# Second feed-forward layer's in-projection by a Strassen product of seven multiplications, from the fifth tile on

## The chip, the core and the metric

The kernel runs on one core of a Trainium2 chip. The core has a matrix engine (TensorE, PE in the profile; PEld is its weight loading), a vector engine (VectorE, DVE), a scalar engine (ScalarE, ACT), a general engine (GpSimd, POOL) and a queue engine that mostly issues transfers (SyncE, SP). POOL and ACT have transfer queues of their own. The metric is the device time of one execution in microseconds (us).

## The reference

One layer of a hybrid decoder on 512 tokens of width 1024, all in float32:

```python
x = x + 0.5 * swiglu_ffn(rmsnorm(x, ffn1_norm), ffn1_w_in, ffn1_w_down)
...
x = x + 0.5 * swiglu_ffn(rmsnorm(x, ffn2_norm), ffn2_w_in, ffn2_w_down)
...
return rmsnorm(h, final_norm)

def swiglu_ffn(x, w_in, w_down):
    a, b = jnp.split(x @ w_in, 2, axis=-1)
    return (jax.nn.silu(a) * b) @ w_down
```

Between the two feed-forward layers (FFN1, FFN2) stand three parallel branches (a state-space model, windowed attention, attention to a memory). The change concerns FFN2, the last stage. Its in-projection multiplies the normalised x (512 x 1024) by a weight matrix of 1024 x 5632: 2816 columns for the gate half a and 2816 for the value half b. The down-projection has 2816 x 1024.

## The kernel before

Activations lie transposed, features on the 128 partitions and the 512 tokens (T) along the rows: `xT[k]` is x's k-th block of 128 features, `uh[k]` and `ul[k]` are the high and low parts (type float32r) of x times the norm's gain. A float32 product is made of three float32r matmuls, high x high, high x low and low x high, which add up in PSUM.

`split` makes the two parts of a block of weights (128 x 1024 numbers): ACT copies it to `wh` (line 124), DVE subtracts to get `wl` (line 125); `split_plain` does the same for activations (lines 143 and 144). `mm_T` (lines 133 to 135) makes one output tile of 128 x 512: 8 blocks of features by three matmuls, 24 matmuls of 512 columns, with a block of weights as the stationary operand and u as the moving one.

The 2816 hidden features are 22 tiles of 128, taken two at a time: `ffn_in(w, f, ...)` makes the tiles f and f + 1. SP loads two chunks of 1 MB through `load_chunk` (two buffers `wraw`), one for the gate and one for the value columns; for each tile there is a product `pa` and a product `pb`, 96 matmuls for the pair. Then comes the gating: DVE multiplies `pa` by the row `rb`, 1 / rms of each token (line 307), ACT takes tanh, DVE forms a (1 + tanh) (310) and multiplies by `pb` (313 in FFN2), and the result is split into `gh` and `gl`, the moving operands of the down-projection. FFN2 leaves r out of the value half; `down2` multiplies by it later, as `rq` = r / 4 of each token.

The tiles form groups, (0, 6), (6, 6), (12, 6), (18, 4) as (first, number). `down2` of a group runs after the first pair of the next group; it accumulates four PSUM tiles `dn0` to `dn3` for each half of the output columns and adds them into `x2n`, x with tokens on the partitions. `natural_x2` makes `x2n` after the first group: 32 transposes on PE (line 1079) and 8 copies on ACT (line 1080).

The program is written in this order, but a scheduler with a priority and a timeline of its own sets each engine's order when the kernel is built. Each engine then works its row in order, and waits where an instruction waits. Transfers of SP's and POOL's queues are issued in the order of those rows too. One line of the main loop is to be kept in mind:

```python
ffn_in(ffn2_w_in, f, fp, g, True)
if f == f0 and pend is not None:
    down2(*pend, False)
```

Of the kernel before, what the change touches and what calls it, by code (L numbers as in the profile page):

```python
# [11 lines left out]
F32 = mybir.dt.float32  # L12
F32R = mybir.dt.float32r
# [7 lines left out]
P = 128  # L21
# [63 lines left out]
def kernel(ctx, tc, x, mem, ffn1_norm, ffn1_w_in, ffn1_w_down, mix_norm, w_in, a_re, a_im, log_dt,  # L85
# [56 lines left out]
    def split_plain(src, h, l, eng=V):  # L142
        S.activation(h, src, AF.Copy)  # L143
        eng.tensor_tensor(l, src, h.bitcast(F32), op=ALU.subtract)  # L144
# [140 lines left out]
    U = list(zip(uh, ul))  # L285


    def ffn_in(w, f, pool, g, late_r):

        begun = w is ffn1_w_in and f == 0  # L290
        if not begun:
            ra = load_chunk(w[0], 0, KD, f * P, 2 * P)
            rbk = load_chunk(w[0], 0, KD, FF + f * P, 2 * P)
        for j in range(2):
            if begun:
                pa, pb = first_ps[(0, j)], first_ps[(FF, j)]
            else:
                pa = ps_tile("mm")
                mm_T(pa, split(ra[:, :, j * P:(j + 1) * P]), U)
                if f + j == 0 and late_r:  # L300
                    norm_sums()
                pb = ps_tile("mm")
                mm_T(pb, split(rbk[:, :, j * P:(j + 1) * P]), U)
            if f + j == 0:
                norm_rows()
            a = pool.tile([P, T], F32, name="ff_a", tag="ff_a", bufs=2)
            V.tensor_tensor(a, pa, rows["r"], op=ALU.mult)  # L307
            t = pool.tile([P, T], F32, name="ff_t", tag="ff_t", bufs=2)
            S.activation(t, a, AF.Tanh, scale=0.5)
            V.scalar_tensor_tensor(a, t, 1.0, a, op0=ALU.add, op1=ALU.mult)  # L310
            b = pool.tile([P, T], F32, name="ff_b", tag="ff_b", bufs=2)
            if late_r:
                V.tensor_tensor(b, a, pb, op=ALU.mult)  # L313
            else:
                V.tensor_tensor(b, pb, rows["r"], op=ALU.mult)
                V.tensor_tensor(b, a, b, op=ALU.mult)
            split_plain(b, *g[f + j])

    def hidden(pool, f0, nf):
        return {f: (pool.tile([P, T], F32R, name="gh", tag="gh", bufs=8),  # L320
# [738 lines left out]
    mid.close()  # L1059


    ps_open("ps_c", 4, "mm")
    ctx.enter_context(ps_stack)
    fp = ctx.enter_context(sb_pool("ffn2"))
    x2 = [fp.tile([P, D], F32, name=f"x2n{r}") for r in range(4)]
    fnb = fp.tile([P, D], F32, name="fnb")
    nc.scalar.dma_start(fnb, bass.AP(tensor=final_norm.tensor, offset=final_norm.offset, ap=[[0, P], [1, D]]))
    ssq = fp.tile([P, 4, 3], F32, name="ssq")
    V.memset(ssq, 0.0)
    rq = fp.tile([P, 4], F32, name="rq")  # L1070
    g = {}

    def natural_x2():
        V.tensor_scalar(rq, r_nat, 0.25, None, op0=ALU.mult)
        for r in range(4):
            for hf in range(2):
                pt = ps_tile("mm")
                for k in range(4):
                    TE.transpose(pt[:, k * P:(k + 1) * P], xT[4 * hf + k][:, r * P:(r + 1) * P], ident)
                S.activation(x2[r][:, hf * T:(hf + 1) * T], pt, AF.Copy)  # L1080

    def down2(f0, nf, last):
        for hf in range(2):
            cols = slice(hf * T, (hf + 1) * T)
            pd = [ps_tile(f"dn{r}", 1) for r in range(4)]
            for f in range(f0, f0 + nf, 4):
                n4 = min(4, f0 + nf - f)
                raw = load_chunk(ffn2_w_down[0], f, n4, hf * T, T)
# [21 lines left out]
            for r in range(4):  # L1110

                for c in ((0, 256), (256, 512)) if last and hf == 1 and r == 3 else ((0, 512),):
                    sub = slice(*c)
                    xr = x2[r][:, hf * T:(hf + 1) * T][:, sub]
                    V.scalar_tensor_tensor(xr, pd[r][:, sub], rq[:, r:r + 1], xr, op0=ALU.mult, op1=ALU.add)
                    if last:
                        junk = fp.tile([P, T], F32, name="junk", tag="junk", bufs=2)
                        n = hf + c[0] // 256
                        S.activation(junk[:, sub], xr, AF.Square, accum_out=ssq[:, r, n:n + 1])
                if last and hf == 0:  # L1120
# [24 lines left out]
    def finish_rows(r, y):  # L1145
        dst = out.rearrange("(j r) d -> r j d", r=4)[r]
        if r < 2:
            G.tensor_scalar(x2[r][:, :T], x2[r][:, :T], y, None, op0=ALU.mult)
        else:
            S.activation(x2[r][:, :T], x2[r][:, :T], AF.Copy, scale=y)  # L1150
        nc.sync.dma_start(dst[:, :T], x2[r][:, :T])
        V.scalar_tensor_tensor(x2[r][:, T:], x2[r][:, T:], y, fnb[:, T:], op0=ALU.mult, op1=ALU.mult)
        nc.sync.dma_start(dst[:, T:], x2[r][:, T:])
# [45 lines left out]
```

## Time and profile before

| | |
|---|---|
| median of 3 runs | 1279.95 us (1278.78 to 1280.48) |
| profiled execution | 1280.05 us |
| its span, first to last instruction | 1278.3 us |
| mean granted TensorE clock | 0.997 |
| first row of the gating of FFN2 on DVE (ff_a, line 307) | 918.51 us |
| PE busy from 1270 us to the end | 0.68 us |

The profile is one execution, taken by the hardware profiler. In a timeline row stand the start and the length of an instruction (us), the engine, the line of the kernel, the operation, "result<-operands", the shape and a count; a bracket at its end is idle time before it and who ended it. Starts that lie closer than the length overlap: the step from start to start is then the price in a row of such instructions. In a row of waits stand who waited, for what, and in total us, how often, and the longest. A row on transfers ends with its count, its size and the median time from issue to landing. Shares of busy time alone say little here, since every stage has its own limit.

### The profile page before, as it was taken

The page shows a single profiled execution, that of the slowest core. Times are in us where ns is not written, and L with a number is a line of the kernel's source. Part 1 is how long each engine was busy: PE and PEld are TensorE (multiplying, and loading weights), DVE is VectorE, ACT ScalarE, POOL GpSimd, SP SyncE. Part 2 cuts the span into 40 slices and gives each one's busy share as a digit, 9 for nine tenths or more (in the row PEclk, how much of TensorE's full clock was granted, in tenths as well). Part 3 has the DMA queues.
Part 4 walks back from the last instruction along what each step waited for, and adds up shares of the span by engine and source line. Part 5 has one row for each costly group of instructions (what it writes and reads, how often), then busy time and mean ns, then how long its engine had stood idle before and what let it go on. Part 6 is the DMA issues. An engine that isn't in the chain of part 4 may idle for free.

```text
span 1278.3 us, 15573 instructions
## 1 busy us (share of the span) xinstructions
PE 1260.2 (99%) x6116; PEld 1036.3 (81%) x6116; DVE 723.1 (57%) x1405; ACT 417.9 (33%) x635; POOL 82.0 (6%) x67
## 2 busy tenths in 40 slices
PE   8999999999999999999999999999999999999997
PEld 6888888788889788898877777888888888888886
DVE  7999456966457477644436544455544354344444
ACT  4322222233335333324424443334323122122233
POOL 3000000000011034400000000002000000000002
PEclk9999999999999999999999999999999999999999
DMA  6233333745237746452227121344231323323221
GB/s 196 89 111 116 131 115 90 190 148 168 84 96 258 227 135 181 146 182 67 66 73 158 42 66 42 99 140 149 83 126 56 116 71 110 115 66 115 92 90 66
DMA packets 152961, 149.34 MB, mean 117 GB/s; under 512 B 27668, under 2 KB 136276, under 8 KB 152596
## 3 DMA queue, kind: packets, MB, share of 16 engines
q1 hardware_dynamic: 129136, 133.48, 33.4%
q10 hardware_dynamic: 23624, 14.61, 3.9%
q8 instruction: 48, 0.79, 0.3%
q0 software_dynamic: 128, 0.26, 0.1%
q14 instruction: 25, 0.20, 0.1%
HBM read 133.35 MB, written 16.16 MB: 117 GB/s over the span
## 4 chain that ended last, share of the span: by engine, by line
PE 93%; DVE 3%; DMA 2%; ACT 1%; issue 0%; SPq 0%; ACTq 0%
PE ps_mm L133 24%; PE ps_mm L134 24%; PE ps_mm L135 24%; PE ps_dn L1107 3%; PE ps_dn L1106 3%; PE ps_dn L1108 3%; PE ps_acc L884 1%; DMA wraw<-in_xattn_w_kv_dram 1%; DVE wl L125 1%; PE ps_mm L822 1%; PE ps_mm L821 1%; PE ps_mm L823 1%; PE ps_tr L877 1%; PE ps_acc L732 1%; DMA wraw<-in_ffn_w_in_dram 1%; PE ps_sc L864 1%
## 5 line engine op out<-in xcount | busy, mean ns | idle before, releaser
L124 ACT ACTIVATE wh<-wraw 128x1024 fp32r<-128x1024 f32 (+2 forms) x242 | 228.5, 946 | 655.0 <-PE ps_mm L134 469.5
L133 PE MATMUL ps_mm<-uh,wh 128*128 128x512 f32 x1024 | 402.2, 393 | 0.8 <-ACT uh L143 0.5
L134 PE MATMUL ps_mm<-ul,wh 128*128 128x512 f32 x1024 | 400.3, 391 | 1.6 <-DVE ul L144 1.6
L135 PE MATMUL ps_mm<-uh,wl 128*128 128x512 f32 x1024 | 400.2, 391 | 0.0
L125 DVE TENSOR_TENSOR wl<-wraw,wh 128x1024 fp32r<-128x1024 f32 (+2 forms) x242 | 269.2, 1114 | 172.8 <-ACT wh L124 166.9
L134 PEld LDWEIGHTS ps_mm<-ul,wh 128*128 128x128 f32 x1024 | 192.9, 188 | 41.7 <-DVE ul L144 1.9
L133 PEld LDWEIGHTS ps_mm<-uh,wh 128*128 128x128 f32 x1024 | 192.6, 188 | 42.0 <-ACT uh L143 0.9
L135 PEld LDWEIGHTS ps_mm<-uh,wl 128*128 128x128 f32 x1024 | 192.6, 188 | 41.2 <-issue 0.7
L307 DVE TENSOR_TENSOR ff_a<-ps_mm,rb 128x512 f32<-128x512 f32 x44 | 30.3, 689 | 89.0 <-PE ps_mm L135 89.0
L1107 PE MATMUL ps_dn<-wl,gh 128*128 128x512 f32 x176 | 70.2, 399 | 0.0
L134 PE MATMUL ps_mm<-gl,wh 128*128 128x512 f32 x176 | 70.1, 398 | 0.0
L133 PE MATMUL ps_mm<-gh,wh 128*128 128x512 f32 x176 | 69.8, 399 | 0.0
L135 PE MATMUL ps_mm<-gh,wl 128*128 128x512 f32 x176 | 69.7, 398 | 0.0
L1106 PE MATMUL ps_dn<-wh,gh 128*128 128x512 f32 x176 | 69.3, 394 | 0.0
L1108 PE MATMUL ps_dn<-wh,gl 128*128 128x512 f32 x176 | 68.8, 392 | 0.0
L217 POOL TENSOR_TENSOR sqacc<-sqacc,sqk 128x512 f32<-128x512 f32 x12 | 20.1, 1677 | 693.9 <-ACT sqk L216 693.8
L313 DVE TENSOR_TENSOR ff_b<-ff_a,ps_mm 128x512 f32<-128x512 f32 x22 | 15.1, 687 | 52.6 <-PE ps_mm L135 52.6
L1106 PEld LDWEIGHTS ps_dn<-wh,gh 128*128 128x128 f32 x176 | 33.0, 188 | 8.6
L133 PEld LDWEIGHTS ps_mm<-gh,wh 128*128 128x128 f32 x176 | 33.0, 188 | 8.1 <-issue 0.2
L135 PEld LDWEIGHTS ps_mm<-gh,wl 128*128 128x128 f32 x176 | 33.0, 188 | 8.0
L1108 PEld LDWEIGHTS ps_dn<-wh,gl 128*128 128x128 f32 x176 | 33.0, 188 | 7.8
L134 PEld LDWEIGHTS ps_mm<-gl,wh 128*128 128x128 f32 x176 | 33.0, 188 | 7.7
(327 smaller groups left out, 1606.1 us busy)
## 6 DMA issues: line engine op xcount, KB each, us to landing
wraw<-in_ffn_w_in_dram SPq DMA_DIRECT2D x42, 1024.0 KB, 5.1
wraw<-in_w_in_dram SPq DMA_DIRECT2D x25, 1024.0 KB, 5.3
wraw<-in_ffn_w_down_dram SPq DMA_DIRECT2D x12, 768.0 KB, 4.8
wraw<-in_ffn_w_down_dram SPq DMA_DIRECT2D x8, 1024.0 KB, 5.1
wraw<-in_ffn_w_down_dram SPq DMA_DIRECT2D x10, 512.0 KB, 3.6
wraw<-in_xattn_w_kv_dram SPq DMA_DIRECT2D x4, 1024.0 KB, 7.4
wraw<-in_ssm_w_glu_dram SPq DMA_DIRECT2D x8, 512.0 KB, 4.7
wraw<-in_w_out_dram SPq DMA_DIRECT2D x4, 1024.0 KB, 5.5
```

The source lines that it names most:

```text
L124: S.activation(h, raw, AF.Copy)
L125: eng.tensor_tensor(l, raw, h.bitcast(F32), op=ALU.subtract)
L133: TE.matmul(ps, h[:, k, :], rhs[k][0], start=first and k == 0, stop=False)
L134: TE.matmul(ps, h[:, k, :], rhs[k][1], start=False, stop=False)
L135: TE.matmul(ps, l[:, k, :], rhs[k][0], start=False, stop=last and k == n - 1)
L217: (V if k == KD - 1 else G).tensor_tensor(rows["sq"], rows["sq"], sq, op=ALU.add)
L307: V.tensor_tensor(a, pa, rows["r"], op=ALU.mult)
L313: V.tensor_tensor(b, a, pb, op=ALU.mult)
L732: TE.matmul(py[:, q * P:(q + 1) * P], lhsT.rearrange("p r c -> p (r c)"), rhs[:, q, :], start=t == 0, stop=t == 2)
L1106: TE.matmul(pd[r], gh[:, tok], h, start=st, stop=False)
L1107: TE.matmul(pd[r], gh[:, tok], l, start=False, stop=False)
L1108: TE.matmul(pd[r], gl[:, tok], h, start=False, stop=en)
```

## The change

For the tiles 4 to 21, nine of the eleven pairs, `fast_in` takes the place of `ffn_in`. The pair's product is seen as a matrix of 2 x 2 blocks: the weights by columns (gate or value) and by half of the 1024 features, u by half of the features and by left and right 256 tokens. Eight products of blocks become seven, with sums of weight blocks (s1 to s4) and of u blocks (t1 to t4), in Winograd's form: t1·s1, u·a11, u·a12, t2·s2, u·s4, t3·s3 and t4·q22, where a11 and a12 are the halves of the gate chunk and q22 is the lower half of the value columns. Each is made for two tiles by 4 blocks of features by three parts: 24 matmuls of 256 columns, 168 for the pair.

- The sums s1 and s3 come from two transfers of 512 KB each: SP loads one block, then POOL's queue adds the other block into the same tile (`accum_op`). The sums s2 and s4 are made by DVE. The blocks s1, s3, q22, s2 and s4 of all pairs share five buffers (`wq`).
- Seven blocks of 128 x 1024 are split for a pair, where four were.
- `combine_u` makes t1 to t4 and their high and low parts once, before tile 4, from x times gain times r; `own_u` writes the parts of u itself again, now with r in them; `natural_x2` moves to this place, and its tiles take the memory of `xT`.
- Partial products lie in halves of PSUM tiles; ACT copies some out (`ff_e` and halves of `ff_a`), DVE adds them. The gate half comes out negated, and tanh and the next step allow for it.
- r is now applied to the value half in `ffn_in`, by one more DVE operation for each tile of f < 4, and `down2` multiplies by the constant 0.25. PSUM has 8 tiles of one kind and no `dn` tiles. `ff_b` goes (`ff_t` is used again), and the load of the final norm moves behind the loop in the program.

```diff
-            a = pool.tile([P, T], F32, name="ff_a", tag="ff_a", bufs=2)
+            a = pool.tile([P, T], F32, name="ff_a", tag="ff_a", bufs=nbuf)
             V.tensor_tensor(a, pa, rows["r"], op=ALU.mult)
             t = pool.tile([P, T], F32, name="ff_t", tag="ff_t", bufs=2)
             S.activation(t, a, AF.Tanh, scale=0.5)
             V.scalar_tensor_tensor(a, t, 1.0, a, op0=ALU.add, op1=ALU.mult)
-            b = pool.tile([P, T], F32, name="ff_b", tag="ff_b", bufs=2)
-            if late_r:
-                V.tensor_tensor(b, a, pb, op=ALU.mult)
-            else:
-                V.tensor_tensor(b, pb, rows["r"], op=ALU.mult)
-                V.tensor_tensor(b, a, b, op=ALU.mult)
-            split_plain(b, *g[f + j])
+            V.tensor_tensor(t, pb, rows["r"], op=ALU.mult)
+            V.tensor_tensor(t, a, t, op=ALU.mult)
+            split_plain(t, *g[f + j])
...
-    ps_open("ps_c", 4, "mm")
+    ps_open("ps_c", 8, "mm")
...
     def natural_x2():
-        V.tensor_scalar(rq, r_nat, 0.25, None, op0=ALU.mult)
-        for r in range(4):
-            for hf in range(2):
+
+        for hf in range(2):
+            pts = []
+            for r in range(4):
                 pt = ps_tile("mm")
                 for k in range(4):
                     TE.transpose(pt[:, k * P:(k + 1) * P], xT[4 * hf + k][:, r * P:(r + 1) * P], ident)
-                S.activation(x2[r][:, hf * T:(hf + 1) * T], pt, AF.Copy)
+                pts.append(pt)
+            for r in range(4):
+                x2[r, hf] = xpool.tile([P, T], F32, name=f"x2n{r}{hf}", tag=f"xT{4 * hf + r}")
+                S.activation(x2[r, hf], pts[r], AF.Copy)
...
+    comb = [{n: fp.tile([P, 4, HT], F32R, name=f"{n}{z}") for n in ("t1", "t2", "t3", "t4")} for z in "hl"]
+    keep = fp.tile([P, 4, 3, HT], F32, name="keep")
+
+    def combine_u():
+
+        for k in range(4):
+            ua = fp.tile([P, T], F32, name="ua", tag="ff_a", bufs=3)
+            V.scalar_tensor_tensor(ua, xT[k], vec[:, 8 + k:9 + k], rows["r"], op0=ALU.mult, op1=ALU.mult)
+            ub = keep[:, k, 1:3].rearrange("p a t -> p (a t)")
+            V.scalar_tensor_tensor(ub, xT[4 + k], vec[:, 12 + k:13 + k], rows["r"], op0=ALU.mult, op1=ALU.mult)
+            S.activation(keep[:, k, 0], ua[:, left], AF.Copy)
+            t = fp.tile([P, T], F32, name="tc", tag="ff_t", bufs=2)
+            t1, t2 = t[:, left], t[:, right]
+            V.tensor_tensor(t1, ua[:, left], ua[:, right], op=ALU.subtract)
+            split_plain(t1, comb[0]["t1"][:, k], comb[1]["t1"][:, k])
+            V.tensor_tensor(t2, ub[:, right], t1, op=ALU.add)
+            S.activation(comb[0]["t2"][:, k], t2, AF.Copy, scale=-1.0)
+            V.scalar_tensor_tensor(comb[1]["t2"][:, k], t2, -1.0, comb[0]["t2"][:, k].bitcast(F32),
+                                   op0=ALU.mult, op1=ALU.subtract)
+            t = fp.tile([P, T], F32, name="tc", tag="ff_t", bufs=2)
+            V.tensor_tensor(t[:, left], ub[:, right], ua[:, right], op=ALU.subtract)
+            split_plain(t[:, left], comb[0]["t3"][:, k], comb[1]["t3"][:, k])
+            V.tensor_tensor(t[:, right], t2, ub[:, left], op=ALU.subtract)
+            split_plain(t[:, right], comb[0]["t4"][:, k], comb[1]["t4"][:, k])
+
+    def own_u():
+
+        for k in range(4):
+            split_plain(keep[:, k, 0], uh[k][:, left], ul[k][:, left])
+        for k in range(4):
+            split_plain(keep[:, k, 1:3].rearrange("p a t -> p (a t)"), uh[4 + k], ul[4 + k])
+
+    def fast_in(w, f, pool, g):
+
+        def quarter(nm):
+            return pool.tile([P, 4, 2 * P], F32, name=nm, tag="wq", bufs=5)
+
+        def src(k0, c0):
+            return w[0][k0 * P:(k0 + 4) * P, c0 + f * P:c0 + (f + 2) * P].rearrange("(k p) c -> p k c", p=P)
+
+        s1 = quarter("s1")
+        nc.sync.dma_start(s1, src(0, FF))
+        nc.gpsimd.dma_start(s1, src(4, FF), accum_op=ALU.add)
+        ra = load_chunk(w[0], 0, KD, f * P, 2 * P)
+        s3 = quarter("s3")
+        nc.sync.dma_start(s3, src(0, FF))
+        nc.gpsimd.dma_start(s3, src(0, 0), accum_op=ALU.add)
+        q22 = quarter("q22")
+        nc.sync.dma_start(q22, src(4, FF))
+        a11, a12 = ra[:, :4, :], ra[:, 4:, :]
+        px = [ps_tile("mm") for _ in range(2)]
+        py = [ps_tile("mm") for _ in range(2)]
+        a = [pool.tile([P, T], F32, name="ff_a", tag="ff_a", bufs=3) for _ in range(2)]
+        e5 = [pool.tile([P, HT], F32, name="ff_e", tag="ff_e", bufs=2) for _ in range(2)]
+
+        def moving(n):
+            if n in comb[0]:
+                return [(comb[0][n][:, k], comb[1][n][:, k]) for k in range(4)]
+            base, half = {"b11": (0, left), "b21": (4, left), "b22": (4, right)}[n]
+            return [(uh[base + k][:, half], ul[base + k][:, half]) for k in range(4)]
+
+        def product(block, n, dst, half, start):
+            h, l = split(block)
+            rhs = moving(n)
+            for j in range(2):
+                o, cols = dst[j][:, half], slice(j * P, (j + 1) * P)
+                for k in range(4):
+                    st = dict(start=start and k == 0, skip_group_check=True)
+                    TE.matmul(o, h[:, k, cols], rhs[k][0], stop=False, **st)
+                    st["start"] = False
+                    TE.matmul(o, h[:, k, cols], rhs[k][1], stop=False, **st)
+                    TE.matmul(o, l[:, k, cols], rhs[k][0], stop=k == 3, **st)
+
+        product(s1, "t1", py, right, True)
+        s2 = quarter("s2")
+        V.tensor_tensor(s2, s1, a11, op=ALU.add)
+        for j in range(2):
+            S.activation(e5[j], py[j][:, right], AF.Copy)
+        product(a11, "b11", px, left, True)
+        for j in range(2):
+            S.activation(a[j][:, left], px[j][:, left], AF.Copy)
+        product(a12, "b21", py, left, False)
+        s4 = quarter("s4")
+        V.tensor_tensor(s4, s2, a12, op=ALU.add)
+        product(s2, "t2", px, left, False)
+        for j in range(2):
+            S.activation(a[j][:, right], px[j][:, left], AF.Copy)
+        product(s4, "b22", py, right, False)
+        product(s3, "t3", px, left, False)
+        for j in range(2):
+            V.tensor_tensor(a[j], a[j], py[j], op=ALU.add)
+        for j in range(2):
+            V.tensor_tensor(px[j][:, right], px[j][:, left], e5[j], op=ALU.add)
+        product(q22, "t4", px, left, False)
+
+        for j in range(2):
+            t = pool.tile([P, T], F32, name="ff_t", tag="ff_t", bufs=2)
+            S.activation(t, a[j], AF.Tanh, scale=-0.5)
+            V.scalar_tensor_tensor(t, t, 1.0, a[j], op0=ALU.subtract, op1=ALU.mult)
+            V.tensor_tensor(t, t, px[j], op=ALU.mult)
+            split_plain(t, *g[f + j])
...
-            pd = [ps_tile(f"dn{r}", 1) for r in range(4)]
+            pd = [ps_tile("mm") for r in range(4)]
...
-                    xr = x2[r][:, hf * T:(hf + 1) * T][:, sub]
-                    V.scalar_tensor_tensor(xr, pd[r][:, sub], rq[:, r:r + 1], xr, op0=ALU.mult, op1=ALU.add)
+                    xr = x2[r, hf][:, sub]
+                    V.scalar_tensor_tensor(xr, pd[r][:, sub], 0.25, xr, op0=ALU.mult, op1=ALU.add)
...
-            ffn_in(ffn2_w_in, f, fp, g, True)
+            if f < 4:
+                ffn_in(ffn2_w_in, f, fp, g, True, 3)
+            else:
+                if f == 4:
+                    combine_u()
+                    natural_x2()
+                    own_u()
+                fast_in(ffn2_w_in, f, fp, g)
             if f == f0 and pend is not None:
                 down2(*pend, False)
-        if pend is None:
-            natural_x2()
         pend = (f0, nf)
+    fnb = fp.tile([P, D], F32, name="fnb", tag="keep")
+    nc.scalar.dma_start(fnb, bass.AP(tensor=final_norm.tensor, offset=final_norm.offset, ap=[[0, P], [1, D]]))
```

DVE around the step from tile 3 to tile 4. In the rows, x2T_* are the blocks of x, keep and ua are u with r, tc the sums of u, t1l to t4l their low parts, and L125 the low part of a weight block. Before, with the last gating of tile 3 first (L313 is its value product):

```order
L313 TENSOR_TENSOR ff_b<-ff_a,ps_mm 128x512
L125 TENSOR_TENSOR wl<-wraw,wh 128x1024
L144 TENSOR_TENSOR gl<-ff_b,gh 128x512
L307 TENSOR_TENSOR ff_a<-ps_mm,rb 128x512
L125 TENSOR_TENSOR wl<-wraw,wh 128x1024
```

Now, with the same step first (L311), the beginning of what stands there:

```order
L311 TENSOR_TENSOR ff_t<-ps_mm,rb 128x512
L144 TENSOR_TENSOR ul_111<-keep,uh_103 128x512
L125 TENSOR_TENSOR wl<-wraw,wh 128x1024
L1100 SCALAR_TENSOR_TENSOR t2l<-tc,t2h 128x256
L144 TENSOR_TENSOR ul_112<-keep,uh_104 128x512
L312 TENSOR_TENSOR ff_t<-ff_a,ff_t 128x512
L1090 SCALAR_TENSOR_TENSOR ua<-x2T_7645,vec,rb 128x512
L144 TENSOR_TENSOR gl<-ff_t,gh 128x512
L1103 TENSOR_TENSOR tc<-keep,ua 128x256
L1105 TENSOR_TENSOR tc<-tc,keep 128x256
L1090 SCALAR_TENSOR_TENSOR ua<-x2T_7683,vec,rb 128x512
L144 TENSOR_TENSOR ul_107<-keep,uh_99 128x256
```

Between the gating of tile 3 and the first gating of the next pair stood one weight split; now the making of u's and t's parts stands there, and goes on for some 25 rows more, with weight splits among them.

DVE at the end of a fast pair, into tile 12 (numbers tell tiles apart; s3_9267 and q22_9270 belong to the pair at 10, s1_9506, s2_9552 and s4_9614 to the pair at 12):

```order
L125 TENSOR_TENSOR wl_9403<-s4_9370,wh_9402 128x1024
L125 TENSOR_TENSOR wl_9431<-s3_9267,wh_9430 128x1024
L1158 TENSOR_TENSOR s2_9552<-s1_9506,wraw_9509 128x1024
L125 TENSOR_TENSOR wl_9463<-q22_9270,wh_9462 128x1024
L1173 TENSOR_TENSOR ff_a_9276<-ff_a_9276,ps_mm_9274 128x512
L1166 TENSOR_TENSOR s4_9614<-s2_9552,wraw_9509 128x1024
L1173 TENSOR_TENSOR ff_a_9277<-ff_a_9277,ps_mm_9275 128x512
L125 TENSOR_TENSOR wl_9525<-s1_9506,wh_9524 128x1024
L1175 TENSOR_TENSOR ps_mm_9272<-ps_mm_9272,ff_e_9278 128x256
L1181 SCALAR_TENSOR_TENSOR ff_t_9490<-ff_t_9490,ff_a_9276 128x512
```

Where a pair had the row of splits and gating shown first, the sum s2 of the next pair, which reads the s1 that POOL's transfer completes, now stands ahead of the split of q22 of the present pair, and the sum s4 ahead of its second ff_a.

POOL's row has these transfers, where nothing stood between FFN2's norm and its last tiles:

```order
L1125 DMA s1_8582<-in_ffn2_w_in_dram 128x4x256
L1129 DMA s3_8587<-in_ffn2_w_in_dram 128x4x256
L1125 DMA s1_9018<-in_ffn2_w_in_dram 128x4x256
L1129 DMA s3_9023<-in_ffn2_w_in_dram 128x4x256
L1125 DMA s1_9262<-in_ffn2_w_in_dram 128x4x256
L1129 DMA s3_9267<-in_ffn2_w_in_dram 128x4x256
```

They go out in this order, one behind the other, each behind the base load of the same tile.

More of the change, by code (lines that the diff above doesn't have):

```diff
@@ L285, with ffn_in @@
     U = list(zip(uh, ul))
-    def ffn_in(w, f, pool, g, late_r):
+    def ffn_in(w, f, pool, g, late_r, nbuf=2):
         begun = w is ffn1_w_in and f == 0
@@ L1059 @@
     mid.close()
-    ps_open("ps_c", 4, "mm")
+    ps_open("ps_c", 8, "mm")
     ctx.enter_context(ps_stack)
     fp = ctx.enter_context(sb_pool("ffn2"))
-    x2 = [fp.tile([P, D], F32, name=f"x2n{r}") for r in range(4)]
-    fnb = fp.tile([P, D], F32, name="fnb")
-    nc.scalar.dma_start(fnb, bass.AP(tensor=final_norm.tensor, offset=final_norm.offset, ap=[[0, P], [1, D]]))
+    HT = T // 2
     ssq = fp.tile([P, 4, 3], F32, name="ssq")
     V.memset(ssq, 0.0)
-    rq = fp.tile([P, 4], F32, name="rq")
     g = {}
+    x2 = {}
+    left, right = slice(0, HT), slice(HT, T)
     def natural_x2():
-        V.tensor_scalar(rq, r_nat, 0.25, None, op0=ALU.mult)
-        for r in range(4):
-            for hf in range(2):
+        for hf in range(2):
+            pts = []
+            for r in range(4):
                 pt = ps_tile("mm")
@@ L1113, in down2 @@
                     sub = slice(*c)
-                    xr = x2[r][:, hf * T:(hf + 1) * T][:, sub]
-                    V.scalar_tensor_tensor(xr, pd[r][:, sub], rq[:, r:r + 1], xr, op0=ALU.mult, op1=ALU.add)
+                    xr = x2[r, hf][:, sub]
+                    V.scalar_tensor_tensor(xr, pd[r][:, sub], 0.25, xr, op0=ALU.mult, op1=ALU.add)
                     if last:
-                        junk = fp.tile([P, T], F32, name="junk", tag="junk", bufs=2)
+                        junk = fp.tile([P, T], F32, name="junk", tag="ff_t", bufs=2)
                         n = hf + c[0] // 256
@@ L1147, in finish_rows @@
         if r < 2:
-            G.tensor_scalar(x2[r][:, :T], x2[r][:, :T], y, None, op0=ALU.mult)
+            G.tensor_scalar(x2[r, 0], x2[r, 0], y, None, op0=ALU.mult)
         else:
[L1150 to L1153, printed above, removed]
+            S.activation(x2[r, 0], x2[r, 0], AF.Copy, scale=y)
+        nc.sync.dma_start(dst[:, :T], x2[r, 0])
+        V.scalar_tensor_tensor(x2[r, 1], x2[r, 1], y, fnb[:, T:], op0=ALU.mult, op1=ALU.mult)
+        nc.sync.dma_start(dst[:, T:], x2[r, 1])
     eps = fp.tile([P, 1], F32, name="eps")
```

## The prediction

> **What bounds the kernel now.** I read the page from its head, then the second FFN's stage as windows, then the stage's waits.
>
> ```profile
> span 1278.3 us, 15573 instructions
> PE 1260.2 (99%) x6116; PEld 1036.3 (81%) x6116; DVE 723.1 (57%) x1405; ACT 417.9 (33%) x635; POOL 82.0 (6%) x67
> 907.00:918.00 11.00, 11.00 (x58) 9.37 (x57) 5.61 (x22) 2.12 (x2) 0.00 (x0) 1.00 0.45 147
> 918.00:967.00 49.00, 49.00 (x217) 40.55 (x217) 25.61 (x32) 15.49 (x20) 0.00 (x0) 1.00 0.27 86
> 967.00:972.00 5.00, 4.71 (x34) 4.01 (x33) 2.51 (x3) 3.10 (x6) 0.00 (x0) 1.00 0.01 2
> 972.00:1030.00 58.00, 58.00 (x257) 47.26 (x256) 22.08 (x26) 15.06 (x19) 0.00 (x0) 1.00 0.28 91
> 1030.00:1270.00 240.00, 240.00 (x1049) 196.56 (x1048) 106.82 (x136) 65.74 (x91) 8.24 (x6) 1.00 0.28 90
> PE ps_mm L1079 <- ACT x2n L1080: 0.3, 1, 0.3
> ACT wh L124 <- PE ps_mm L134: 150.0, 39, 5.3
> DVE wl L125 <- ACT wh L124: 64.6, 60, 8.6
> ```
>
> The columns of a window row are length, then busy time of PE, weight loads, DVE, ACT and POOL, then the granted clock, the DMA share and GB/s. PE is busy in every microsecond of the stage at clock 1.00, and its only wait there for another engine is 0.3 us in the transposes. ACT and DVE wait for PE or for each other: from 1030 to 1270 DVE works 106.82 of 240 us. So the stage costs what its matmuls cost, and the change has to shorten PE's row without making PE wait. The profiled run took 1280.05 us, 1.75 more than its span; the median of the three runs is 1279.95, so sums made against 1280.05 need no correction.
>
> **Term 1, the matmuls.** A pair of tiles is now 4 x 24 = 96 matmuls of 512 columns; for nine of the eleven pairs it becomes 7 x 24 = 168 of 256 columns. Both widths run back to back in this trace:
>
> ```profile
> 929.65 0.39 PE L134 MATMUL ps_mm<-ul,wh 128*128 128x512 f32 x1
> ...
> 936.00 0.39 PE L135 MATMUL ps_mm<-uh,wl 128*128 128x512 f32 x1
> 475.81 0.28 PE L822 MATMUL ps_mm<-wl,uh 128*128 128x256 f32 x1
> 475.93 0.19 PEld L821 LDWEIGHTS ps_mm<-wh,uh 128*128 128x128 f32 x1
> ...
> 481.32 0.28 PE L823 MATMUL ps_mm<-wh,ul 128*128 128x256 f32 x1
> ```
>
> The first two matmul rows are 28 steps apart (29 matmuls in that stretch): 6.35/28 = 0.2268 us. The other two are 46 steps apart (47 matmuls): 5.51/46 = 0.1198 us, each with a weight load of its own of 0.19 us that lies beside its neighbour. A pair goes from 96 x 0.2268 = 21.77 to 168 x 0.1198 = 20.13 us, 1.64 less; nine pairs give **-14.8 us**. An eighth of the products goes, but halving the width loses 0.0064 us per matmul, so only 7.5% of the time goes. This bounds the gain: 1280.05 - 14.8 = 1265.3 if nothing else costs anything.
>
> Going by the Trainium skill, "TensorE: Matmul & The Clock Gate", section "Wait — 56ns, not 53.3ns?", back-to-back matmuls stand N/2.4 GHz plus about 2.5 ns apart, and a pair would save about 2.4 us, nine pairs 21. The two measured steps are each about 11 ns longer than that rule; 14.8 goes by the rows.
>
> **Term 2, the switch at f=4.** Four combinations of the normalised u, their high and low parts, and new high and low parts of u itself have to be made before the first fast pair. They cannot start earlier than the normaliser is there, and the overwritten u parts not before f=3's last matmuls have read the old ones. DVE's price list, from five instructions that follow each other without a gap:
>
> ```profile
> 412.84 0.75 DVE L636 SCALAR_TENSOR_TENSOR u<-xT,vec,rb 128x512 f32<-128x512 f32 x1
> 413.51 0.42 DVE L144 TENSOR_TENSOR mvs<-ps_mm,mvs 128x256 fp32r<-128x256 f32 x1
> 413.84 0.68 DVE L144 TENSOR_TENSOR ul<-u,uh 128x512 fp32r<-128x512 f32 x1
> 414.44 1.22 DVE L125 TENSOR_TENSOR wl<-wraw,wh 128x1024 fp32r<-128x1024 f32 x1
> 415.57 0.68 DVE L144 TENSOR_TENSOR ul<-u,uh 128x512 fp32r<-128x512 f32 x1
> 968.87 2.34 PE L1079 MATMUL ps_mm<-ident,x2T 128*128 128x128 f32 x20
> 971.50 1.63 PE L1079 MATMUL ps_mm<-ident,x2T 128*128 128x128 f32 x12 [0.28 <-ACT x2n L1080]
> 970.86 3.51 ACT L1080 ACTIVATE x2n<-ps_mm 128x512 f32<-128x512 f32 x7
> ```
>
> From start to start: 0.67 for 512 columns times a vector and a row, 0.33 for 256, 0.60 for 512, 1.13 for 1024. After f=3's last matmul DVE still has, up to the low part of the last t2 that the product t2·s2 waits for: 5 instructions of 512 (3.0), 2 of ua (1.3), 2 weight splits (2.3), 30 of 256 columns (9.9), together 16.5 us. One wait stands in that row: the low gating part waits for its high part, which ACT makes behind the copies of the transposed x, and ACT's pitch there is 3.51/7 = 0.50 us; laid out this is 1.6 us. Some twenty hand-overs DVE to ACT to DVE of the small parts, interleaved, I take at 1.5 in all. That is 19.6 us. PE can meanwhile run the 32 transposes, 2.34 + 1.63 = 4.0 plus some 0.3 between, now ahead of the first product, and 68 matmuls that need no late part, 8.1: 12.5 us. PE loses 19.6 - 12.5 = **7 us**. Lower end: no waits at all, 16.5 - 12.5 = 4. Upper end: the durations 0.68, 0.75, 1.22, 0.42 in place of the pitches, 19.9 + 1.6 + 1 - 12.5 = 10. I take the middle, since the pitches are what such rows show.
>
> **Term 3, the seams of the fast pairs.** DVE now has per pair 7 weight splits and 2 sums of 1024, 8 operations of 512 and 2 of 256: 9 x 1.13 + 8 x 0.60 + 2 x 0.33 = 15.6 of 20.1 us, against 4 x 1.13 + 8 x 0.60 = 9.3 of 21.8 before. It stays below PE, but its row is crowded at the end of a pair: in the 5.8 us of b22 and t3 it splits q22 (which can begin 1.2 us into b22, after ACT's split of 1.06 below), adds ff_a, makes the next s4, adds ff_a again (not before b22 ends) and then splits the next s1: 0.60 + 1.22 after b22's end at best, about 3.0 by the row, and PE asks for it with the third matmul after t3, 2.88 + 0.24 = 3.1 after b22's end. So there is hardly slack, and I put **1.5 us** over all eight seams; from 0 to 8 (1 us each, two 512-column operations late).
>
> ```profile
> 941.69 1.06 ACT L124 ACTIVATE wh<-wraw 128x1024 fp32r<-128x1024 f32 x1 [3.86 <-PE ps_mm L134]
> 942.65 0.62 ACT L309 ACTIVATE ff_t<-ff_a 128x512 f32<-128x512 f32 x1
> ```
>
> ACT has 7 such splits, 6 copies of 256, 2 tanh and 2 high parts: 7 x 1.0 + 6 x 0.3 + 4 x 0.55 = 11 of 20.1 us, never the bound. Loads on SP's queue grow from 2 to 2.5 MB a pair, plus 1 MB that POOL adds; at 0.28 DMA share for 90 GB/s, 3.5 MB in 20.1 us (174 GB/s) are a share of about 0.55. The extra gating operation for f<4 (0.60, four times) lies where DVE has room; the dropped scaling of r and the smaller reorderings in earlier stages I put at nothing, since PE is busy there throughout; if that cover failed they cost under 1 us.
>
> **Term 4, the accumulating transfers.** None is in the trace. The next s1 gets its slot when the present s1 is split, about when the present pair's first product starts; the base load lands after some 5 us; then POOL's transfer adds the other half. DVE's sum s2 of the next pair, which stands ahead of q22's split, asks for it about 14.4 us into the pair: a window of some **9 us**. Nearest rows:
>
> ```profile
> wraw<-in_ffn_w_in_dram SPq DMA_DIRECT2D x42, 1024.0 KB, 5.1
> wraw<-in_ffn_w_down_dram SPq DMA_DIRECT2D x10, 512.0 KB, 3.6
> wraw<-in_ssm_w_glu_dram SPq DMA_DIRECT2D x8, 512.0 KB, 4.7
> bre<-in_ssm_b_re_dram POOLq DMA_DIRECT2D x1, 128.0 KB, 4.8
> dcol<-in_ssm_d_dram POOLq DMA_DIRECT2D x1, 2.0 KB, 3.0
> ```
>
> Below: 3.6 us, as a plain load of 512 KB. Above: POOL's 128 KB in 4.8 us taken four times, 19 us. I take 7: POOL's base of 3.0, plus twice the 1.8 us that separate 128 KB from 2 KB there. So it is hidden: **0**, and at the upper end (19 - 9) = 10 us at each of the four seams that no down-projection lies in (into f=10, 12, 16 and 18), 40 us.
>
> Going by the Trainium skill, "DMA: Bandwidth & Descriptors", section "Anatomy of one DMA — SWDGE (gpsimd) path", a transfer from POOL's queue takes about 2.0 us plus its bytes at 436 GB/s, so 512 KB would take an estimated 3.2 us and sit well inside the window. The row of 4.8 us for 128 KB, where this rule gives 2.3, does not agree, and the page does not say what adding costs.
>
> **Sum.** 1280.05 - 14.8 + 7 + 1.5 + 0 = 1273.75: forecast **1274 us**, 0.5% faster; by the ends of terms 2 and 3 alone 1269.3 to 1283.3.
>
> **The rivals.**
> *The sums land late (slower).* POOL's transfer takes over 9 us from base to landing. DVE then stands at s2 of the next pair, behind it q22's split and both ff_a sums, and PE stops in t4 and t1. At 12 us: 4 x 3 = 12, so 1286; at 15 us: 24, 1298; at 19 us: 1314. For: POOL's few rows are slow for their bytes, and adding has to read the target too. Against: 7 us by the nearest rows. It decides from 10.6 us, where 4 x 1.6 eats the gain. Chance 0.22.
> *DVE is the bound at the switch and at the seams.* Terms 2 and 3 at their upper parts, 9 and 6 us: 1280. For: 15.6 of 20.1 us busy, with in-order rows. Against: DVE has 4.5 us to spare per pair. Chance 0.16.
> *The switch costs little, seams nothing.* DVE's rows overlap ACT's as well as PE's: 1265.3 + 4 = 1269. Chance 0.1.
> *The narrow step is shorter here than at 476 us.* If 256 columns took just half of 512's step, 0.1134, a pair would take 19.1 us, nine pairs would save 25 and the sum would be 1264. For: the widths are one to two. Against: 46 steps of the same shape and type say 0.1198. The Trainium skill's rule above leans this way. Chance 0.02.
> *The forecast*, 1271 to 1277: 0.5.
>
> **How the numbers follow.** A measurement of this kernel can tell about 0.2% from no change, 1277.4 to 1282.5. Faster: 0.5 + 0.1 + 0.02, less the forecast's upper edge, plus the lower edge of the DVE rival: 0.62. Same: most of the DVE rival and the shortest delays of the sums: 0.17. Slower: 0.21, nearly all of it late sums. The range that leaves out 2 in 10 goes from 1267 (the cheap switch) to 1291 (a sum of 13 us).
>
> **What the profile of the changed kernel would show.** Right: 256-column matmuls of the fast pairs 0.12 apart and 1512 of them; one gap of some 7 us in PE's row at the switch, released by DVE's small low parts; PE else over 97% busy from there to the end; accumulating transfers under 9 us. Wrong: a step other than 0.12 moves term 1 by 1.5 us per ns; PE waiting for the split of s1 after every t3 means that term 3 is too small; DVE waiting for an s1 from POOL means the first rival; a gain over 15 us would mean that the old step was longer than the rows say.

## The result and the profile after

| | before | changed |
|---|---|---|
| median | 1280.22 us (1278.78 to 1280.75, 4 runs) | 1271.99 us (1270.98 to 1273.29, 4 runs) |
| profiled execution | 1280.05 us | 1273.29 us |
| its span | 1278.3 us | 1271.5 us |

The ratio is 0.9938, with a 95% interval from 0.9921 to 0.9955: 0.6% faster, 2 us below the forecast of 1274. The changed kernel's profiled execution is the longest of its four, so stages are compared below by lengths inside the traces, and kernels by their medians.

The head of the changed kernel's page, and windows over its last stage: from the end of tile 3's matmuls the transposes, the switch, the first fast pair, and all the rest up to the last matmul. Columns as in the prediction.

```profile
span 1271.5 us, 17256 instructions
PE 1249.1 (98%) x6764; PEld 1058.3 (83%) x6764; DVE 800.6 (63%) x1519; ACT 474.9 (37%) x744; POOL 104.8 (8%) x85
...
948.33:951.70 3.37, 3.37 (x32) 3.37 (x31) 3.37 (x6) 2.89 (x7) 0.00 (x0) 1.00 0.54 88
951.70:967.32 15.62, 12.80 (x76) 11.60 (x75) 15.20 (x38) 12.28 (x31) 0.00 (x0) 0.78 0.32 104
967.32:990.00 22.68, 22.12 (x185) 21.92 (x184) 17.97 (x21) 13.15 (x20) 2.57 (x2) 1.00 0.69 165
990.00:1262.00 272.00, 272.00 (x1782) 249.10 (x1781) 170.72 (x210) 114.55 (x168) 21.74 (x17) 1.00 0.48 126
```

From 990 us on PE is busy in every microsecond. All that is lost lies between 951.70 and 990, most of it in the 15.62 us of the switch, of which DVE is busy for 15.20. All waits of PE for other engines in the stage:

```profile
PE ps_mm L1151 <- ACT uh L143: 1.7, 2, 1.5
PE ps_mm L1151 <- ACT wh L124: 1.0, 2, 0.6
PE ps_mm L1153 <- DVE ul L144: 0.7, 1, 0.7
```

They make 3.4 us. The rest of the loss hides in PE's busy time: the granted clock of the switch's window is 0.78. The timeline of PE there, start and length of each instruction, with its idle time in brackets:

```profile
948.10 0.39 PE L135 MATMUL ps_mm<-uh,wl 128*128 128x512 f32 x1
948.33 3.65 PE L1075 MATMUL ps_mm<-ident,x2T 128*128 128x128 f32 x32
951.74 0.36 PE L1151 MATMUL ps_mm<-t1h,wh 128*128 128x256 f32 x1
...
955.67 0.50 PE L1151 MATMUL ps_mm<-uh,wh 128*128 128x256 f32 x2 [1.54 <-ACT uh L143]
956.84 0.39 PE L1153 MATMUL ps_mm<-ul,wh 128*128 128x256 f32 x1 [0.67 <-DVE ul L144]
...
963.48 0.41 PE L1154 MATMUL ps_mm<-t2h,wl 128*128 128x256 f32 x1
963.70 0.42 PE L1151 MATMUL ps_mm<-t2h,wh 128*128 128x256 f32 x1
963.91 0.41 PE L1154 MATMUL ps_mm<-t2h,wl 128*128 128x256 f32 x1
...
966.84 0.28 PE L1153 MATMUL ps_mm<-t2l,wh 128*128 128x256 f32 x1
...
967.32 0.28 PE L1151 MATMUL ps_mm<-uh,wh 128*128 128x256 f32 x1
```

From 948.33 to 967.32 PE has 3.41 us of transposes and 72 matmuls of 256 columns, 8.63 us at 0.1198; it takes 18.99. So it loses 18.99 - 12.04 = **6.95 us**. Some of its matmuls stand 0.21 us apart, not 0.12: behind the gaps at 954 to 957 us the granted clock was 0.52 from 959 to 965 us. The whole stretch as a window, and rows of DVE in it:

```profile
948.33:967.32 18.99, 16.17 (x106) 14.97 (x105) 18.57 (x43) 15.17 (x37) 0.00 (x0) 0.82 0.36 101
...
949.63 0.68 DVE L311 TENSOR_TENSOR ff_t<-ps_mm,rb 128x512 f32<-128x512 f32 x1
...
961.40 1.22 DVE L125 TENSOR_TENSOR wl<-s,wh 128x1024 fp32r<-128x1024 f32 x1
...
966.22 0.41 DVE L1100 SCALAR_TENSOR_TENSOR t2l<-tc,t2h 128x256 fp32r<-128x256 f32 x1
966.56 0.41 DVE L144 TENSOR_TENSOR t4l<-tc,t4h 128x256 fp32r<-128x256 f32 x1
968.19 2.45 DVE L125 TENSOR_TENSOR wl<-s,wh 128x1024 fp32r<-128x1024 f32 x2 [1.22 <-ACT wh L124]
```

DVE works 18.57 of these 18.99 us and rests only at the end. The low part of the last t2, with which the sum of the prediction ended, runs from 966.22 to 966.63 us, and PE's first matmul with it starts at 966.84. So the slow clock, which lies ahead of it, cost 0.2 us here at most: a faster PE would have waited for that part instead. At 967.32 PE has done all matmuls of this pair that need t1 or t2.

The tightest seam, into tile 12: SP issues the base load of s1, POOL the adding transfer, DVE makes s2 from it and splits s1. The row on transfers is that of POOL's queue in the window from 1050 to 1060 us, with its time to landing at the end.

```profile
1050.60 0.37 SPq L1124 DMA_DIRECT2D s<-in_ffn_w_in_dram  x1
1054.68 1.28 POOL L1125 DMA_DIRECT2D s<-in_ffn_w_in_dram  x1 [9.07 <-DMA s<-in_ffn_w_in_dram]
s<-in_ffn_w_in_dram POOLq DMA_DIRECT2D x1, 512.0 KB, 9.4
1049.35 1.22 DVE L125 TENSOR_TENSOR wl<-s,wh 128x1024 fp32r<-128x1024 f32 x1
1064.46 1.23 DVE L1158 TENSOR_TENSOR s<-s,wraw 128x1024 f32<-128x1024 f32 x1
1069.50 1.22 DVE L125 TENSOR_TENSOR wl<-s,wh 128x1024 fp32r<-128x1024 f32 x1
```

DVE's two splits of an s1 are 20.15 us apart: that is the period of a fast pair, 168 x 0.1199. The sum landed at 1054.68 + 9.4 = 1064.1, and DVE came for it at 1064.46. It did not wait, but by 0.4 us only. Into tile 18 it is nearly as tight: issued at 1148.48, landed after 9.3 us, and DVE came for it at 1158.33.

### The profile page after: what moved, and what is told of

Read it like the earlier page. It is cut to its first block, busy times and chain, and to the rows that moved or that the text cites. A ratio compares the mean times of both kernels' runs of the same rounds, so it can differ in the third digit from the quotient of the medians.

```text
span 1271.5 us, 17256 instructions
## 1 busy us (share of the span) xinstructions
PE 1249.1 (98%) x6764; PEld 1058.3 (83%) x6764; DVE 800.6 (63%) x1519; ACT 474.9 (37%) x744; POOL 104.8 (8%) x85
## 4 chain that ended last, share of the span: by engine, by line
PE 92%; DVE 4%; DMA 2%; ACT 1%; issue 0%; SPq 0%; ACTq 0%
PE ps_mm L133 19%; PE ps_mm L135 19%; PE ps_mm L134 19%; PE ps_mm L1151 5%; PE ps_mm L1153 5%; PE ps_mm L1154 5%; PE ps_mm L1209 3%; PE ps_mm L1211 3%; PE ps_mm L1210 3%; DMA wraw<-in_xattn_w_kv_dram 1%; PE ps_acc L880 1%; DVE wl L125 1%; PE ps_mm L818 1%; PE ps_mm L817 1%; PE ps_mm L819 1%; PE ps_tr L873 1%
## 5 line engine op out<-in xcount | busy, mean ns | idle before, releaser
L125 DVE TENSOR_TENSOR wl<-wraw,wh 128x1024 fp32r<-128x1024 f32 (+2 forms) x224 | 248.0, 1109 | 130.4 <-ACT wh L124 124.3
L133 PE MATMUL ps_mm<-uh,wh 128*128 128x512 f32 x736 | 289.9, 394 | 0.9 <-ACT uh L143 0.5
L134 PE MATMUL ps_mm<-ul,wh 128*128 128x512 f32 x736 | 288.2, 392 | 1.6 <-DVE ul L144 1.6
L135 PE MATMUL ps_mm<-uh,wl 128*128 128x512 f32 x736 | 288.5, 392 | 0.0
L134 PEld LDWEIGHTS ps_mm<-ul,wh 128*128 128x128 f32 x736 | 138.7, 188 | 30.6 <-DVE ul L144 1.9
L125 DVE TENSOR_TENSOR wl<-s,wh 128x1024 fp32r<-128x1024 f32 x36 | 44.0, 1224 | 43.1 <-ACT wh L124 43.1
L1210 PE MATMUL ps_mm<-wl,gh 128*128 128x512 f32 x176 | 69.4, 394 | 0.0
L1211 PE MATMUL ps_mm<-wh,gl 128*128 128x512 f32 x176 | 69.1, 394 | 0.0
L1209 PE MATMUL ps_mm<-wh,gh 128*128 128x512 f32 x176 | 66.9, 395 | 0.0
L1151 PE MATMUL ps_mm<-uh,wh 128*128 128x256 f32 x216 | 61.1, 285 | 2.3 <-ACT uh L143 1.7
L1153 PE MATMUL ps_mm<-ul,wh 128*128 128x256 f32 x216 | 61.4, 285 | 0.7 <-DVE ul L144 0.7
L1154 PE MATMUL ps_mm<-uh,wl 128*128 128x256 f32 x216 | 61.0, 284 | 0.0
```

Of the source, the lines that this page charges most:

```text
L125: eng.tensor_tensor(l, raw, h.bitcast(F32), op=ALU.subtract)
L133: TE.matmul(ps, h[:, k, :], rhs[k][0], start=first and k == 0, stop=False)
L134: TE.matmul(ps, h[:, k, :], rhs[k][1], start=False, stop=False)
L135: TE.matmul(ps, l[:, k, :], rhs[k][0], start=False, stop=last and k == n - 1)
L1151: TE.matmul(o, h[:, k, cols], rhs[k][0], stop=False, **st)
L1153: TE.matmul(o, h[:, k, cols], rhs[k][1], stop=False, **st)
```

## The experiments

All times are medians; the kernel before ran beside each group, 1279.3 us (1277.98 to 1280.91) beside the work left out, the first cover, the double adding and the sums on DVE, and 1280.09 (1277.72 to 1283.42) beside the other four. The question behind the first group: is the loss DVE's, and how near are the seams to costing something?

**The work at the switch left out.**

```diff
-            base, half = {"b11": (0, left), "b21": (4, left), "b22": (4, right)}[n]
+            base, half = {"b11": (0, left), "b21": (4, left), "b22": (4, right), "t1": (0, left),
+                          "t2": (4, left), "t3": (0, right), "t4": (4, right)}[n]
...
-                    combine_u()
                     natural_x2()
-                    own_u()
```

> The work at the switch is left out: the four sums of u, their high and low parts and the new parts of u are not made, and the fast products use u's own parts (without r) in their place. Theory (DVE's 16.5 us of instructions behind tile 3's last matmul hold PE up for 7 us, and nothing else at the switch does): 1272.0 - 7 = 1265 us, 1264 to 1267, with PE busy from tile 3 to tile 4 and the clock at 1.00 there. Rival (the transposes, ACT's eight copies out of PSUM or the halved clock seen there are the cause, and DVE only fills the time): 1270 to 1272.

Measured: 1264.22 us (1262.98 to 1264.88). The window from the end of tile 3:

```profile
947.37:967.00 19.63, 19.63 (x168) 19.63 (x167) 11.57 (x12) 13.29 (x22) 1.29 (x1) 1.00 0.61 149
```

PE has no idle time and full clock, with the transposes and ACT's copies of them out of PSUM still there. So the loss is that of the sums and parts of u, 1271.99 - 1264.22 = 7.8 us, good to about 1 us, since the kernel before was 0.9 us faster beside this group. The traces say 7.55: from the start of tile 3's last matmul to that of the last of all it is 1254.63 - 947.14 = 307.49 us here and 1263.14 - 948.10 = 315.04 in the changed kernel. The transposes and these copies fall as causes. The slow clock went together with the gaps, so this run alone can't part it from them; the row at 966.84 us above does. The run also leaves out ACT's share of the sums and parts; that DVE sets the time is read from its row.

**The switch covered.** All work is done; the first group has four tiles, and its down-projection stands ahead of the first fast pair.

```diff
+    groups = [(0, 4), (4, 6), (10, 6), (16, 6)]
...
                 if f == 4:
                     combine_u()
                     natural_x2()
                     own_u()
+                    down2(*pend, False)
                 fast_in(ffn2_w_in, f, fp, g)
-            if f == f0 and pend is not None:
+            if f == f0 and pend is not None and f != 4:
```

> All the work is done, but the first group has four tiles (groups 4, 6, 6, 6) and its down-projection stands between the switch and the first fast pair: 96 matmuls of 512 columns, some 22 us, that need none of the sums. Theory (the 7 us are DVE's, and 22 us of other matmuls cover its 19 us): 1265 us, 1264 to 1267, no PE gap over 1 us and the clock at 1.00. Rival (the down-projection needs DVE too, for 4 weight splits and 8 additions, and its first matmuls wait for the gating of tile 3, which stands in the same DVE row): half of the gain or less, 1269 to 1272.

Measured: 1268.42 us (1267.84 to 1269.96), 3.6 less than the changed kernel, half of what the theory said, and between the two expectations. The windows from tile 3's end, and behind the last matmul:

```profile
947.05:1000.00 52.95, 51.73 (x341) 47.12 (x340) 44.78 (x74) 29.59 (x55) 3.85 (x3) 1.00 0.50 132
1000.00:1256.20 256.20, 256.20 (x1734) 237.15 (x1732) 162.85 (x198) 112.80 (x169) 21.75 (x17) 1.00 0.51 131
1256.20:1267.00 10.80, 0.18 (x1) 0.00 (x0) 5.72 (x21) 3.36 (x11) 3.62 (x2) 0.67 0.52 194
```

The cover works: PE idles for 1.2 us in all and keeps its clock. From tile 3's last matmul to the last of all it takes 5.9 us less than the changed kernel (1255.99 - 946.82 = 309.17). But 10.6 us follow the last matmul (it starts at 1255.99, the span ends at 1266.6) where 8.4 followed before (1263.14, 1271.5): with a last group of six, the last four sums into the rows of the output start within 4.2 us of each other on DVE (1252.24 to 1256.41) where they took 6.4 (1257.31 to 1263.75), so that four products of the final norm are left behind the last sum where two were.

**The same with a last group of four.** This tests that reading. Against the first cover, only the groups change:

```diff
-    groups = [(0, 4), (4, 6), (10, 6), (16, 6)]
+    groups = [(0, 4), (4, 6), (10, 4), (14, 4), (18, 4)]
```

> As the kernel with the covered switch (1268.4), but in groups of 4, 6, 4, 4, 4. Theory (that kernel had no gap at the switch, and gave 2.2 us back behind the last matmul, 10.6 us against 8.4, because a last group of six finishes its four blocks of rows in the last 5.5 us instead of one by one): 1266.2 us, 1265 to 1267.5, with 8.4 us behind the last matmul. Rival (the 2.2 us have another cause, or the fifth down-projection costs as much): 1268 or more.

Measured: **1266.75 us** (1265.22 to 1269.09), 0.9900 of the kernel before (0.9884 to 0.9916). Its last matmul starts at 1258.82 and its span ends at 1267.3, 8.5 us later, so the last group's size is what the 2.2 us hang on. From tile 3's last matmul to the end of the span it takes 318.0 us, where the first cover takes 319.8 and the changed kernel 323.4. The times of the two covers overlap, but by its median this is the fastest kernel of the study that does all the work.

**s1 added to twice.** One more line behind the first adding transfer, so that s1 is complete later; the block that it adds is not part of the product.

```diff
         nc.gpsimd.dma_start(s1, src(4, FF), accum_op=ALU.add)
+        nc.gpsimd.dma_start(s1, src(4, FF), accum_op=ALU.add)
```

> POOL adds the second block into s1 twice, one transfer behind the other (s1 is then no longer the sum that the product needs). In the changed kernel the adding transfer took 6.2 us from issue to landing in the median, and at the seam into tile 12 DVE asked for s1 9.8 us after the issue. Theory (hidden with 3.6 us to spare, and the first rival's price is right from there on): two in a row take about 12.5 to 14 us, 3 to 4 us late at four seams, of which DVE's slack there takes about 1: 4 x 2 to 3 = 8 to 12 us more, 1280 to 1284. Rival (a late s1 costs PE nothing because the weight splits run two products ahead): 1272 to 1274.

Measured: 1294.88 us (1291.69 to 1296.48), 22.9 more, about twice what was expected. DVE's and PE's rows at the seam into tile 12, and DVE's waits for these transfers from 1000 to 1200 us:

```profile
1073.89 1.23 DVE L1159 TENSOR_TENSOR s<-s,wraw 128x1024 f32<-128x1024 f32 x1 [8.22 <-DMA s<-in_ffn_w_in_dram]
1075.03 0.58 PE L1152 MATMUL ps_mm<-t1h,wh 128*128 128x256 f32 x1 [3.01 <-ACT wh L124]
1079.77 0.58 PE L1155 MATMUL ps_mm<-t1h,wl 128*128 128x256 f32 x1 [3.52 <-DVE wl L125]
DVE s L1159 <- DMA s<-in_ffn_w_in_dram: 21.2, 4, 8.2
```

The first rival's mechanism is real: DVE stands 8.2 us at s2, and PE waits 6.5 us behind it. The four waits are at the seams that the prediction named, into tiles 10, 12, 16 and 18. Its size was underestimated because the expectation took the median of 6.2 us for a transfer that takes 9.4 in the changed kernel at this seam, and 11.2 here. And the lengths of 0.58 in place of 0.39 show matmuls at half clock after each such gap: the clock is 0.85 from 1055 to 1090 us, which adds to the waits. Between the same two matmuls this trace is 24.5 us longer than the changed kernel's (1286.34 - 946.81 = 339.53); PE's waits, 20.0 us against 3.4, make 16.6 of it, and the rest lies in matmuls that stand further apart.

**Both sums on DVE, no adding transfers.**

```diff
-        nc.gpsimd.dma_start(s1, src(4, FF), accum_op=ALU.add)
+        p1 = quarter("p1")
+        nc.sync.dma_start(p1, src(4, FF))
+        V.tensor_tensor(s1, s1, p1, op=ALU.add)
...
-        nc.gpsimd.dma_start(s3, src(0, 0), accum_op=ALU.add)
+        V.tensor_tensor(s3, s3, ra[:, :4, :], op=ALU.add)
```

> No adding transfers: s1's second block is loaded by SP into a buffer of its own and DVE makes both sums, s1 and s3, two more operations of 1024 columns for a pair (1.13 us each), 17.9 of 20.1 us. Theory (POOL's adding is worth something because DVE's row is crowded at a pair's end): PE waits 0.3 to 1.2 us at each of eight seams, 1274 to 1281. Rival (DVE's spare 4.5 us take the two sums anywhere): 1271 to 1273.

Measured: 1283.96 us (1281.72 to 1285.36), slower than the kernel before (1.0035, 1.0023 to 1.0047) and outside both expectations. Two places in its timelines:

```profile
913.60 1.23 DVE L1127 TENSOR_TENSOR s<-s,p 128x1024 f32<-128x1024 f32 x1 [3.56 <-DMA p<-in_ffn_w_in_dram]
916.75 0.46 PE L232 MATMUL ps_mm<-dg,ones 128*128 128x128 f32 x2 [3.18 <-DVE dg L231]
979.88 0.39 PE L1156 MATMUL ps_mm<-t3h,wl 128*128 128x256 f32 x1 [1.89 <-DVE wl L125]
```

The first is what had not been thought of: the sum for the pair at tile 4 was put into DVE's row ahead of the norm's own chain, waited there for its load, and PE stood 3.2 us for the norm. Behind tile 3 the stage takes 6.9 us longer than in the changed kernel (1273.78 - 951.82 = 321.96 us between the same two matmuls, against 315.04), with six more gaps of 0.17 to 1.9 us, where PE waits for splits: its waits grow from 3.4 to 7.8 us, and where the other 2.5 us lie was not traced. Most of what is left of the 12 us lies ahead of that matmul, which comes 3.7 us later. DVE also stands 10.8 us behind tile 3, in eight waits, for the loads of the extra block, which is the sixth of a pair in five buffers. How much belongs to DVE's added work, how much to these waits and how much to the order that came out was not separated, so the run doesn't price the two sums alone.

**The adding transfers left out.** s1 and s3 hold one block each instead of a sum.

```diff
-        nc.gpsimd.dma_start(s1, src(4, FF), accum_op=ALU.add)
...
-        nc.gpsimd.dma_start(s3, src(0, 0), accum_op=ALU.add)
```

> POOL's eighteen adding transfers are left out, so s1 and s3 hold one block each instead of a sum. Theory (the transfers are hidden: 3.6 us to spare at the tightest seam, and no wait of DVE, ACT or PE for them in the changed kernel's trace): 1271 to 1273 us, as the changed kernel. Rival (they hold up other loads on the shared transfer engines or PE's operands): 2 us or more faster, 1270 or less.

Measured: 1272.51 us (1271.62 to 1272.92), no different from the changed kernel, though the room at the tightest seam was 0.4 us and not the 3.6 that the expectation gave; from tile 3's last matmul to the last it takes 315.00 us, where the changed kernel takes 315.04. The eighteen transfers cost nothing as they stand.

**The last four pairs plain again.**

```diff
-            if f < 4:
+            if f < 4 or f >= 14:
                 ffn_in(ffn2_w_in, f, fp, g, True, 3)
```

> Only the pairs at 4, 6, 8, 10 and 12 use seven products; the last four pairs (14 to 20) go back to the plain in-projection with 96 matmuls of 512 columns (which multiplies by r once more, since u already has r in it). Theory (each fast pair saves 21.77 - 20.15 = 1.62 us of matmuls and its seams cost nothing): 1272.0 + 4 x 1.62 = 1278.5 us. Rival (a fast pair loses part of its gain at its seams, in down-projections next to it, or gains more than the matmul steps say): outside 1277.0 to 1280.0.

Measured: 1277.25 us (1276.43 to 1279.3), 5.3 more than the changed kernel and in the lower part of what the theory allowed. Within the traces it fits closely: between the same two matmuls it takes 1267.08 - 945.55 = 321.53 us, 6.49 more than the changed kernel, or 1.62 a pair.

**Width alone.** The kernel before, with each output tile from tile 4 on made in two halves of 256 columns.

```diff
+        for c in (slice(0, T // 2), slice(T // 2, T)):
+            for k in range(KD):
...
+                TE.matmul(ps[:, c], h[:, k, :], uh[k][:, c], stop=False, **st)
+                st["start"] = False
+                TE.matmul(ps[:, c], h[:, k, :], ul[k][:, c], stop=False, **st)
+                TE.matmul(ps[:, c], l[:, k, :], uh[k][:, c], stop=k == KD - 1, **st)
```

> The kernel before, with nothing changed but the width: from tile 4 on each output tile is made as two halves of 256 columns, 192 matmuls for a pair in place of 96. Theory (the step is 0.2268 us at 512 columns and 0.1198 at 256, weight loads stay beside them): 192 x 0.1198 - 96 x 0.2268 = 1.23 us for a pair, nine pairs 11.1: 1279.3 + 11.1 = 1290.4 us. Rival of the formula with a fixed 2.5 ns (0.2158 and 0.1092 us): 0.25 us a pair, 1281.6. Rival with halves at half the step: 1279.3.

Measured: 1291.73 us (1289.55 to 1292.85), 11.6 more than the kernel before beside it. The first and the last of 52 matmuls in a row of its trace:

```profile
975.78 0.28 PE L298 MATMUL ps_mm<-ul,wh 128*128 128x256 f32 x1
...
981.90 0.28 PE L298 MATMUL ps_mm<-ul,wh 128*128 128x256 f32 x1
```

51 steps in 6.12 us are 0.1200 each, as the older rows at 476 us said. The rule that the prediction weighed (the Trainium skill, "TensorE: Matmul & The Clock Gate", section "Wait — 56ns, not 53.3ns?") gives an estimated 2.2 us in place of 11.6; the measurement decides against it for these float32r matmuls.

## Why the prediction was right, step by step

- **What bounds the kernel.** Right: PE alone, before and after, but for some 20 us behind tile 3, in which DVE is the bound.
- **Term 1, -14.8 us.** Right. The period of a fast pair is 20.15 us (forecast 20.13), the slope by leaving four pairs out is 1.62 a pair by the traces (1.3 by the medians), nine pairs 14.6. The run on width alone shows the other half of the reckoning: halving the width costs 11.6 us for these pairs, so an eighth fewer multiplications made these products only 7.5% shorter.
- **Term 2, +7 us.** Right in cause; the size, 6.95 us by the timeline and 7.55 to 7.8 with the work left out, came out partly because errors cancel. DVE's instructions stood as laid out: by their steps, the same 39 take 16.9 us (949.63 to 966.55), against 16.5. But the waits in that row, put at 1.6 + 1.5 us, are about 0.4, while DVE came to the row only 1.3 us behind tile 3's last matmul, and PE needed another 0.8 us behind it. That is 19.0 us in place of 19.6; PE's other work is 12.04 in place of 12.5. The sign that was named did not show either: not one gap of some 7 us released by small low parts, but four gaps of 2.8 us in all, the longest of them ended by ACT's high part of u, and slow matmuls between them. The halved clock was not in the sum. From 956 to 959 us and from 959 to 965 it is 0.83 and 0.52 in the changed kernel, and 0.50 and 0.96 in the one without adding transfers, whose tile 3 ends 1 us earlier, while the length behind tile 3 is the same within 0.04 us. With the row at 966.84 us, that shows DVE as the bound there and the slow clock beside it.
- **Term 3, +1.5 us.** Too large by 0.7: the only gap in the fast pairs behind the switch is 0.56 us, in the first one, and costs 0.8 by the starts of the matmuls around it (two steps take from 976.29 to 977.35 us); behind it PE waits at no seam. The value was an allowance inside a range from 0 to 8, and DVE's crowded row just fits: in it s1 is split at 1069.50 us, one period after 1049.35.
- **Term 4, 0.** Right, but nearer to the edge than it said. The median is 6.2 us (value taken 7, window 9); the transfer that matters takes 9.4 of a window of 9.8. Four of the eighteen took 9.2 to 9.4, over the 9 us that the prediction had named as a sign of being right; a window shorter by more than 0.4 us would have made DVE wait.
- **The rival that the sums land late.** Its mechanism was shown by adding twice. Its price, one us for each us by which DVE waits at a seam, is about right, but not by its own reckoning: DVE's four waits make 21.2 us and the kernel lost 22.9, but PE's gaps are shorter than DVE's waits (6.5 us for 8.2 at tile 12), and the slower matmuls behind them, which the price did not have, make up for it.
- **The sum.** 1280.05 - 14.6 + 7.8 (the switch and the 0.8 us) = 1273.25, against 1273.29 in the profiled run; the median is 1.3 lower. That the profiled run fits so closely is partly chance: from tile 3's last matmul to the last of all it gained 8.4 us (1270.29 - 946.88 = 323.4, to 315.0), of which the terms make 6.8, the transposes 0.7 (3.41 us in one piece where they took 4.1 in two) and 0.9 stay unassigned, and it came to the end of tile 3 1.2 us later than the kernel before (948.33 against 947.1 us). Among kernels whose changes lie behind that point it was 945.78 (the last pairs plain) to 949.56 us (the cover with a last group of four), so 1.2 us there say nothing.

## What to carry to other kernels

Where one engine sets the time and a trick trades its work for others', price the trick by steps of the new shape taken from the same trace, not by counting multiplications: an eighth less work was 7.5% less time. The one-time preparation cost as much as half of the nine pairs' gain, and a stretch of work that doesn't need it, put in front of the first use, gave 5 us of it back for a few changed lines. Before handing a sum to a transfer, find the one place where its landing is due soonest and read the duration there: the median said 3.6 us to spare, that place had 0.4.

## What the runs showed of the hardware

- Two gaps of PE of 1.54 and 0.67 us close together were followed by several microseconds at half the granted clock: 0.52 from 959 to 965 us in the changed kernel, with steps of 0.21 us for 256 columns; between and behind the stalls of 3.01 and 3.52 us in the kernel that adds twice it was 0.50 from 1077 to 1083 us. Single gaps left it at 1.00 up to 2.33 us: of 0.6 us in the covered kernels, of 1.89 with the sums on DVE (980 to 986 us), of 2.33 in the kernel that adds twice (1052.4 to 1060 us). A gap of 2.95 us in the latter was followed by 0.72 from 1159 to 1165 us. So a stall of PE that no other bound hides costs more than its length: 16.6 us more of waits came with 24.5 us more of time there. The Trainium skill, "TensorE: Matmul & The Clock Gate", section "What's actually happening", has the clock fall to a half after an idle window of about 3.4 us; the half agrees, but PE was not idle for so long in the changed kernel.
- A transfer of 512 KB that adds into SBUF took 5.8 to 9.4 us from issue to landing, 1.28 us of it on POOL, where plain loads of 512 KB on SP's queue had 3.5 to 5.3 in the median. The long ones at the seams into tiles 12 and 18 (9.4 and 9.3) ran beside a load of 1 MB that took 8.8 and 8.3 us itself; that the two slow each other was not tried.
